# The projection weights' loads on ScalarE's DMA queue instead of SyncE's

## The chip, the cores and the metric

One core of a Trainium2 chip runs the whole kernel: TensorE (PE) multiplies, VectorE (DVE), ScalarE (ACT) and GpSimd (POOL) work beside it, and DMA transfers are issued by SyncE (SP) or ScalarE, each with a queue of its own. Every engine takes its instructions in the order in which the program gives them out. The metric is the device time of one execution in microseconds.

## The reference

One layer of a hybrid decoder block over 512 tokens of width 2048, in float32:

```python
h = _rms_norm(x, norm1_g[l])
proj = h @ w_in[l]
aq, ak, av, bu, bg, cq, ck, cv = jnp.split(proj, splits, axis=-1)
...                                   # per-head RMS norms of q and k
out_a = _dilated_mixture(aq, ak, av)  # 8 heads x 64, three dilated windows
out_b = _conformer_conv(bu, bg, ...)  # GLU, causal depthwise conv (31), LayerNorm, swish
out_c, _ = _band_attention(cq, ck, cv, C_WINDOW - 1, sinks=c_sinks[l])  # 16 q heads, 2 kv heads
x = x + jnp.concatenate([out_a, out_b, out_c], axis=-1) @ w_out[l]
h2 = _rms_norm(x, norm2_g[l])
x = x + (jax.nn.silu(h2 @ w_gate[l]) * (h2 @ w_up[l])) @ w_down[l]
```

The input projection has 3840 columns, that is 30 tiles of 128.

## The kernel before, in words

Every product is made of three: each float32 operand is split into a high part (a cast to the matmul's reduced float32, `F32R`) and the low rest, and high x high, high x low and low x high are summed in PSUM (`mm3`, L315 to L317).

**Weight units.** The weights pass through the kernel in units of 128 x 1024. A unit's way has three steps. `pump` loads it into one of a few raw buffers (`nc.sync.dma_start`, L254); `split_up_to` makes the high part with a cast on ScalarE (L286) and puts the subtraction that makes the low part into the list `lows`; `lows_now` gives that subtraction to VectorE (L264). Once a unit is split its raw buffer counts as free, and the next load into it must wait until the subtraction has read it. `next_unit` is called where PE is about to use unit u: it casts unit u + 2 (`SPLIT_AHEAD`), into one of three buffers, which PE must have released. `pump` fills raw buffers up to a limit, five of them before unit 20 (`RAW_EARLY`) and eight after (`RAW_BUFS`; seven names in use here).

**The stages.** A head part (the first four tiles, sharing the loads of x) takes the first 50 us. Then `project` makes the other 26 tiles of the input projection, two units each, in the order of `PROJ`. While PE multiplies, every second of the eight k-tiles of a unit advances a clock (`ticks.tick()`); work that was put down for a tick is given out there. In this way the attention heads, the convolution's taps (L526) and the norms run between the projections. When all tiles are made, `late` is set and the output projection begins (residual add at L1019, loads of x at L1004); after that come the gate, up and down products.

**The small transfers.** What follows a projection tile moves data across partitions through SP's queue: per-head sums of squares go out in four parts and come back (`head_scales`, L595 and L600); halves of q are copied to the other partitions, called twins (L638, L639); the scales of k go out, come back spread (L663, L669), and k's high and low parts are copied in eight transfers (L692); v goes out turned and comes back (L702, L708). On POOL, the returned sums become scales at L608 to L610, v is scaled at L713, and the heads of kind c get their probabilities spread by selects (L819, L822). Scores are at L763 and L764, transposes of probabilities at L799 (c) and L865 (a), the weighing of values at L889 and L890; ScalarE's exponentials are at L784 (c) and L838 (a), its copies out of PSUM at L578, L805, L871 and L898; VectorE's norm of kind a is at L845 to L849, its low parts at L810 and L876.

**Where a load is given out.** In `project`, `lows_now` is called at the fourth of a unit's eight k-tiles. It gives the subtraction to VectorE, and since `late_lows` is set it calls `pump` right after, so one weight load stands in SP's queue at the middle of each unit, ahead of whatever the following ticks put there. The kernel writes the order out by hand; nothing is moved by a scheduler.

Of the kernel before, what the change touches and what calls it, by code (L numbers as in the profile page):

```python
# [52 lines left out]
RAW_BUFS = 8  # L53
RAW_EARLY = 5
# [62 lines left out]
def kernel(ctx: ExitStack, tc: tile.TileContext, xT, wi, wo, wgu, wd, cst_in, outT):  # L117
    nc = tc.nc
# [22 lines left out]
    def bank(name, cols=T, pool="banks"):  # L141
        return psum[pool].tile([P, cols], F32, name=name, tag="b")
# [11 lines left out]
    def take(buf, key, n=1024):  # L154
        assert buf not in held
        held[buf] = key
        raws[key] = (wp.tile([P, 1024], F32, name=f"w{key}", tag=f"raw{buf}", bufs=1), n)
        return raws[key][0]
# [81 lines left out]
    splits = {}  # L240
    at = {"entry": 0, "split": 0, "use": 0}

    def pump(limit, most=99):
        while at["entry"] < len(entries) and len(raws) < limit and entries[at["entry"]][0] not in held and most:
            most -= 1
            buf, key, parts = entries[at["entry"]]
            if len(parts[0].shape) == 3:
                n = 4 * parts[0].shape[-1]
                nc.sync.dma_start(take(buf, key, n)[:, :n].rearrange("p (n f) -> p n f", n=4), parts[0])
                at["entry"] += 1  # L250
                continue
            t, o = take(buf, key, sum(p.shape[-1] for p in parts)), 0
            for part in parts:
                nc.sync.dma_start(t[:, o:o + part.shape[-1]], part)  # L254
                o += part.shape[-1]
            at["entry"] += 1


    lows, late_lows = [], []

    def lows_now():
        while lows:
            fn, *args = lows.pop(0)
            fn(*args)  # L264
        if late_lows:
            pump(RAW_EARLY if at["use"] <= 20 else RAW_BUFS)

    def split_up_to(i):
        while at["split"] <= min(i, len(works) - 1):
            key, last, eng = works[at["split"]]  # L270
            t, n = drop(key) if last else raws[key]
            u = at["split"]
            hi = wp.tile([P, 1024], F32R, name=f"wh{u}", tag="hi", bufs=SPLIT_BUFS)
            lo = wp.tile([P, 1024], F32R, name=f"wl{u}", tag="lo", bufs=SPLIT_BUFS)
            if eng == "moves":

                near = psum["high"].tile([P, 1024], F32R, name=f"wn{u}", tag="h")
                src = t[:, :n].rearrange("p (n f c) -> p f n c", n=4, c=P)
                by = lambda x: x[:, :n].rearrange("p (f n c) -> p f n c", n=4, c=P)
                nc.scalar.copy(by(near), src)  # L280
                nc.scalar.copy(by(hi), src)
                nc.vector.tensor_sub(by(lo), src, by(near).bitcast(F32))
            elif eng or "high" not in psum:
                eng = eng or nc.vector

                (nc.vector.tensor_copy if u == 0 else nc.scalar.copy)(hi[:, :n], t[:, :n])  # L286
                lows.append((eng.tensor_sub, lo[:, :n], t[:, :n], hi[:, :n].bitcast(F32)))
                if not late_lows:
                    lows_now()
            else:  # L290
                near = psum["high"].tile([P, 1024], F32R, name=f"wn{u}", tag="h")
                nc.scalar.copy(near[:, :n], t[:, :n])
                nc.scalar.copy(hi[:, :n], t[:, :n])
                lows.append((nc.vector.tensor_sub, lo[:, :n], t[:, :n], near[:, :n].bitcast(F32)))
                if not late_lows:
                    lows_now()
            splits[u] = (hi, lo)
            at["split"] += 1

    def sums_now():  # L300
        for fn in sums.pop(at["use"], ()):
            fn()

    def next_unit():
        sums_now()
        u = at["use"]
        at["use"] += 1
        lows_now()
        split_up_to(u + SPLIT_AHEAD)
        if not lows:  # L310
            pump(RAW_EARLY if u < 20 else RAW_BUFS, 2 if works[u][2] == "moves" else 99)
        return splits.pop(u)

    def mm3(out, wh, wl, xh, xl, start, stop):
        nc.tensor.matmul(out, wh, xh, start=start, stop=False)  # L315
        nc.tensor.matmul(out, wh, xl, start=False, stop=False)  # L316
        nc.tensor.matmul(out, wl, xh, start=False, stop=stop)  # L317
# [11 lines left out]
    for k in range(X_AHEAD):  # L329
        load_first(k)  # L330
        if k < 4 or k % 2 == 0:
            pump(k + 2 if k < 4 else k // 2 + 4)
# [109 lines left out]
    for k in range(KT):  # L442
# [5 lines left out]
        if k == 0:  # L448

            at["use"] = 2  # L450
            first = [splits.pop(u) for u in range(2)]
        elif k < 4 or k % 2 == 0:
            wh, wl = next_unit()
            o = 0
# [32 lines left out]
    def project(name):  # L487
        b = bank(name, pool="tiles")
        for half in range(2):
            wh, wl = next_unit()  # L490
            for kk in range(8):
                k = 8 * half + kk
                s = slice(kk * P, (kk + 1) * P)
                mm3(b, wh[:, s], wl[:, s], h_hi[k], h_lo[k], k == 0, k == KT - 1)
                if kk == 3:
                    lows_now()
                if kk % 2 == 1:
                    ticks.tick()
        return b
# [436 lines left out]
    mix, late = {}, []  # L936
# [34 lines left out]
    for name in PROJ[HEAD4:]:  # L971
        kind, what, j = name[0], name[1], name[2:]
        if name == PROJ[-2]:
            for n, row in enumerate(ROWS[:8]):
                ticks.after(6 + n, split_mix, row)
        b = project(name)
        if kind == "b":
            ticks.after(0, glu_u if what == "u" else glu, int(j), b)
            continue
        if kind == "c":  # L980
            box = Heads(shared) if j else shared
        else:
            box = boxes.setdefault(j, {})
        if what == "k":
            do_k(box, b, name, 1 if kind == "c" else 0)
        elif what == "v":
            do_v(box, b, name)
        else:
            do_q(box, b, name)
        if what == "q":  # L990
            if kind == "a":
                boxes.pop(j)
            attention(kind, box, mix, kind + j, (int(j), int(j) + 8) if kind == "c" else None)
# [82 lines left out]
    for half in range(2):  # L1076
        for i, n in enumerate(OUT_ORDER[half]):
            if half == 1 and i == 2:
                open_banks(banks=2, high=2)
            b = bank(f"o{half}_{n}", pool="tiles")  # L1080
            wh, wl = next_unit()
            for kk in range(8):
                k = 8 * half + kk
                row = ROWS[k]
                while row not in m_hi:
                    ticks.tick()
                s = slice(kk * P, (kk + 1) * P)
                mm3(b, wh[:, s], wl[:, s], m_hi[row], m_lo[row], kk == 0, kk == 7)
                if kk % 4 == 3 or half == 0 and kk % 2 == 1:
                    ticks.tick()  # L1090
            ticks.after(0, residual, n, b, half)
            if half == 0:
                load_x(i + 2)
        for row in ROWS[8 * half:8 * half + 8]:
            if half == 0:
                m_hi.pop(row), m_lo.pop(row)
# [263 lines left out]
    class Down:  # L1360
# [74 lines left out]
        def sum(self, i, k, a):  # L1435
            return self.g, i, k, a
# [140 lines left out]
```

## Time and profile before

| | us |
|---|---|
| median of 3 runs | 1875.88 |
| lowest and highest | 1874.54, 1877.67 |
| profiled execution | 1874.93 |
| its span | 1873.2 |
| PE busy | 1857.4 |

In rows of the profile, a line begins with its start (or, for groups, with the kernel's line), and square brackets tell how long the engine idled before it and what ended that. `wh` and `wl` are the high and low parts of a weight unit, `w` its raw buffer. Names such as `cq4d` are the data of head tile cq4 in memory, `cq4t` the same read back, `ak1h` a twin of k's high part. SPq and ACTq are the DMA issues of the two queues; the bytes move later, and a transfer's own time is given in the chain of waits as DMA.

### The profile page before, as it was taken

The page shows a single profiled execution, that of the slowest core. Times are in us where ns is not written, and L with a number is a line of the kernel's source. Part 1 is how long each engine was busy: PE and PEld are TensorE (multiplying, and loading weights), DVE is VectorE, ACT ScalarE, POOL GpSimd, SP SyncE. Part 2 cuts the span into 40 slices and gives each one's busy share as a digit, 9 for nine tenths or more (in the row PEclk, how much of TensorE's full clock was granted, in tenths as well). Part 3 has the DMA queues.
Part 4 walks back from the last instruction along what each step waited for, and adds up shares of the span by engine and source line. Part 5 has one row for each costly group of instructions (what it writes and reads, how often), then busy time and mean ns, then how long its engine had stood idle before and what let it go on. Part 6 is the DMA issues. An engine that isn't in the chain of part 4 may idle for free.

```text
span 1873.2 us, 28281 instructions
## 1 busy us (share of the span) xinstructions
PE 1857.4 (99%) x9566; PEld 1588.8 (85%) x9566; DVE 1449.9 (77%) x2295; ACT 1327.3 (71%) x1835; POOL 1155.5 (62%) x838
## 2 busy tenths in 40 slices
PE   9999999999999999999999999999999999999998
PEld 7888878877888888888888888888888888888887
DVE  6779878989689777777777777777777777777767
ACT  6355644553457888888888888888888877778775
POOL 0136543110003887877878778787777778879775
PEclk9999999999999999999999999999999999999999
DMA  7353244453333445465554655546456967666645
GB/s 271 86 153 91 85 133 118 114 142 134 115 140 113 136 159 163 153 191 168 173 162 154 194 162 174 162 154 195 148 167 235 328 215 238 216 223 230 205 136 113
DMA packets 227649, 311.34 MB, mean 166 GB/s; under 512 B 86320, under 2 KB 138672, under 8 KB 227504
## 3 DMA queue, kind: packets, MB, share of 16 engines
q1 hardware_dynamic: 227360, 309.52, 52.1%
q8 instruction: 76, 1.25, 0.3%
q14 instruction: 69, 0.57, 0.1%
q10 hardware_dynamic: 144, 0.01, 0.0%
HBM read 246.65 MB, written 54.42 MB: 161 GB/s over the span
## 4 chain that ended last, share of the span: by engine, by line
PE 89%; DVE 5%; DMA 2%; SPq 2%; POOL 1%; issue 1%; ACT 0%; POOLq 0%; DVEq 0%
PE out L1172 46%; PE out L1431 7%; PE out L1430 7%; PE out L1432 7%; PE o L315 3%; PE o L317 3%; PE o L316 3%; PE cq L315 1%; PE cq L317 1%; PE cq L316 1%; DVE wl L264 1%; PE in L315 1%; PE in L317 1%; PE in L316 1%; DVE y L526 1%
## 5 line engine op out<-in xcount | busy, mean ns | idle before, releaser
L1172 PE MATMUL out<-h,wh 128*128 128x512 f32 x2464 | 588.6, 391 | 0.0
L1172 PEld LDWEIGHTS out<-h,wh 128*128 128x128 f32 x2464 | 453.1, 188 | 87.1
L1172 PEld LDWEIGHTS out<-h,wl 128*128 128x128 f32 x2464 | 315.9, 191 | 12.0
L1172 PE MATMUL out<-h,wl 128*128 128x256 f32 x2464 | 319.7, 283 | 0.0
L1430 PE MATMUL out<-wh,a 128*128 128x512 f32 x620 | 240.6, 388 | 0.0
L1432 PE MATMUL out<-wh,a 128*128 128x512 f32 x620 | 240.6, 388 | 0.0
L1431 PE MATMUL out<-wl,a 128*128 128x512 f32 x620 | 240.6, 388 | 0.0
L286 ACT CAST wh<-w 128x1024 fp32r<-128x1024 f32 (+2 forms) x94 | 96.8, 1031 | 123.2 <-PE o L316 54.9
L264 DVE TENSOR_TENSOR wl<-w,wh 128x1024 fp32r<-128x1024 f32 (+2 forms) x95 | 113.6, 1196 | 34.2 <-ACT wh L286 34.0
L1430 PEld LDWEIGHTS out<-wh,a 128*128 128x128 f32 x620 | 116.5, 188 | 23.8
L1432 PEld LDWEIGHTS out<-wh,a 128*128 128x128 f32 x620 | 116.5, 188 | 23.8
L1431 PEld LDWEIGHTS out<-wl,a 128*128 128x128 f32 x620 | 116.5, 188 | 23.7
L1440 DVE TENSOR_TENSOR y<-y,out 128x512 f32<-128x512 f32 x164 | 106.4, 683 | 25.6 <-PE out L1432 23.7
L526 DVE SCALAR_TENSOR_TENSOR y<-bu,cst,y 128x511 f32<-128x511 f32 (+14 forms) x120 | 89.1, 743 | 0.8
L315 PE MATMUL o<-mh_c,wh 128*128 128x512 f32 x128 | 51.3, 400 | 2.5 <-DVE xr L1019 2.5
L315 PE MATMUL cq<-hh,wh 128*128 128x512 f32 x128 | 50.3, 393 | 0.0
L317 PE MATMUL o<-mh_c,wl 128*128 128x512 f32 x128 | 50.0, 391 | 0.0
L316 PE MATMUL o<-ml_c,wh 128*128 128x512 f32 x128 | 50.0, 390 | 0.0
L316 PE MATMUL cq<-hl,wh 128*128 128x512 f32 x128 | 49.9, 390 | 0.0
L317 PE MATMUL cq<-hh,wl 128*128 128x512 f32 x128 | 49.9, 390 | 0.0
L182 POOL TENSOR_TENSOR w('s', 'g0')_5692<-w('21', 'g0')_5538,w('22', 'g0')_5536 128x1024 f32<-128x1024 f32 x1 | 2.5, 2454 | 68.9 <-DVE wl L264 68.9
L431 POOL TENSOR_TENSOR lvr<-lvv,nhalf 128x4 f32<-128x4 f32 x1 | 1.9, 1920 | 67.9 <-DVE lvv L430 67.9
(3052 smaller groups left out, 4949.6 us busy)
## 6 DMA issues: line engine op xcount, KB each, us to landing
od<-a SPq DMA_DIRECT2D x154, 256.0 KB
a<-od SPq DMA_DIRECT2D x154, 256.0 KB
w<-in_wi SPq DMA_DIRECT2D x58, 512.0 KB
w<-in_wo SPq DMA_DIRECT2D x32, 512.0 KB
x<-in_xT SPq DMA_DIRECT2D x16, 256.0 KB
xr<-in_xT SPq DMA_DIRECT2D x16, 256.0 KB
x2d<-xr SPq DMA_DIRECT2D x16, 256.0 KB
z<-x2d SPq DMA_DIRECT2D x64, 64.0 KB
```

The source lines that it names most:

```text
L182: nc.gpsimd.tensor_add(out[:, :n], raws[key[a]][0][:, :n], raws[key[b]][0][:, :n])
L264: fn(*args)
L286: (nc.vector.tensor_copy if u == 0 else nc.scalar.copy)(hi[:, :n], t[:, :n])
L315: nc.tensor.matmul(out, wh, xh, start=start, stop=False)
L316: nc.tensor.matmul(out, wh, xl, start=False, stop=False)
L317: nc.tensor.matmul(out, wl, xh, start=False, stop=stop)
L526: nc.vector.scalar_tensor_tensor(yconv[j][:, i:], hconv[j][:, :T - i], c, yconv[j][:, i:], op0=ALU.mult, op1=ALU.add)
L1172: nc.tensor.matmul(out, lhs[:, s], rhs, start=begin, stop=x is xs[-1] and low == flip[0], skip_group_check=True)
L1430: nc.tensor.matmul(b[:, lo:hi], x[:, high], wh[:, s], start=start, stop=False, skip_group_check=True)
L1431: nc.tensor.matmul(b[:, lo:hi], x[:, high], wl[:, s], start=False, stop=False, skip_group_check=True)
L1432: nc.tensor.matmul(b[:, lo:hi], x[:, low], wh[:, s], start=False, stop=last, skip_group_check=True)
L1440: getattr(eng, op)(t, t, src)
```

## The change

In `project`, `next_unit` is called with ScalarE's queue. It then pumps at once, before the cast of unit u + 2, and gives the loads to ScalarE's queue; the pump at the middle of the unit is left out until `late` is set. The head part and the stages after the projections load through SP as they did, and every small transfer stays on SP's queue.

```diff
-    def pump(limit, most=99):
+    def pump(limit, most=99, queue=nc.sync):
...
             for part in parts:
-                nc.sync.dma_start(t[:, o:o + part.shape[-1]], part)
+                queue.dma_start(t[:, o:o + part.shape[-1]], part)
...
             fn(*args)
-        if late_lows:
-            pump(RAW_EARLY if at["use"] <= 20 else RAW_BUFS)
+        if late_lows and late:
+            pump(RAW_BUFS)
...
-    def next_unit():
+    def next_unit(queue=None):
         sums_now()
         u = at["use"]
         at["use"] += 1
+        if queue:
+            pump(RAW_EARLY if u < 20 else RAW_BUFS, queue=queue)
         lows_now()
         split_up_to(u + SPLIT_AHEAD)
-        if not lows:
+        if not queue and not lows:
             pump(RAW_EARLY if u < 20 else RAW_BUFS, 2 if works[u][2] == "moves" else 99)
         return splits.pop(u)
...
         for half in range(2):
-            wh, wl = next_unit()
+            wh, wl = next_unit(nc.scalar)
```

## The prediction

> **What bounds the kernel now.** I read the profile's page first, its busy times: one engine fills the span.
>
> ```profile
> PE 1857.4 (99%) x9566; PEld 1588.8 (85%) x9566; DVE 1449.9 (77%) x2295; ACT 1327.3 (71%) x1835; POOL 1155.5 (62%) x838
> ```
>
> So only PE's idle time can be won, 1873.2 - 1857.4 = 15.8 us, and only that of the stage the change touches. Next, the busy times by stretch (start:end, length, then PE, PEld, DVE, ACT, POOL).
>
> ```profile
> 62.00:224.00 162.00, 161.40 (x812) 136.81 (x812) 131.56 (x254) 83.41 (x183) 66.74 (x102) 1.00 0.37 107
> 224.00:430.00 206.00, 197.35 (x970) 164.41 (x969) 173.93 (x389) 99.55 (x189) 59.20 (x90) 1.00 0.45 124
> 430.00:545.00 115.00, 115.00 (x531) 95.43 (x530) 89.68 (x163) 51.64 (x83) 1.92 (x1) 1.00 0.37 131
> ```
>
> The projections with the attention heads between them fill 62 to about 400 us. PE idles 0.6 us in the first stretch, 8.65 us in the second and none in the third. At most 9.2 us, 0.5% of the time, can be won. The view of waits on PE names all of it (us, times, longest):
>
> ```profile
> PE o L315 <- DVE xr L1019: 2.5, 2, 1.6
> PE c7o L890 <- POOL c7pl L822: 2.1, 2, 1.8
> PE c4o L890 <- POOL c4pl L822: 1.8, 2, 1.3
> PE c6s L763 <- DMA cq<-cq6l: 1.2, 1, 1.2
> PE a1o L890 <- DVE a1pl L876: 1.0, 1, 1.0
> PE c0s L764 <- DMA ckl<-cklo: 0.6, 1, 0.6
> ```
>
> None of them is a wait for weights. What the change can shorten stands in SP's own waits in the same stage, where a weight load (L254) is held until VectorE has subtracted from the buffer that it overwrites, with every small transfer behind it held too:
>
> ```profile
> SPq L254 <- DVE wl L264: 109.9, 24, 7.9
> ```
>
> **The change part by part.**
>
> **Small transfers freed, c7.** The chain of waits and the timelines of SP, POOL and VectorE show how the 2.1 us at c7o come about.
>
> ```profile
> 222.32 1.51 DMA ak2d<-ak2p
> 226.19 3.23 DMA ak2t<-ak2d
> 239.64 3.68 DMA cq4t<-cq4d
> ```
>
> ```profile
> 225.65 0.35 SPq L254 DMA_DIRECT2D w<-in_wi  x1
> 239.00 0.53 SPq L254 DMA_DIRECT2D w<-in_wi  x1
> ```
>
> ```profile
> 229.49 0.20 POOL L608 TENSOR_TENSOR ak2wide<-ak2t 128x8 f32<-128x8 f32 x1 [1.67 <-DMA ak2t<-ak2d]
> 243.39 0.29 POOL L608 TENSOR_TENSOR cq4r<-cq4t 128x8 f32<-128x8 f32 x1 [7.59 <-DMA cq4t<-cq4d]
> ```
>
> ```profile
> 232.74 0.21 DVE L657 STREAM_TRANSPOSE ak2wide<-ak2wide 128x32 f32<-128x32 f32 x1 [0.90 <-POOL ak2wide L610]
> ```
>
> The write ak2d has landed at 222.32 + 1.51 = 223.83, but its reading back starts at 226.19, behind a weight load. Without it the read starts 2.4 us earlier. POOL can use 1.67 us of that (its idle time) and VectorE 0.9 (its own). From VectorE's transpose on, SP issues back to back up to cq4t, and a second weight load sits in front of that: 239.64 - 239.00 = 0.64 us more. Issued 1.5 us earlier, cq4t also lands sooner: 3.68 us behind 512 KB, 1.51 for a transfer without them, so 0 to 2.2 off. I take 1.2, nearer to the 3.23 and 3.68 of this kind of read. POOL, which stood 7.59 us for it, then hands c7pl over 2.7 us (1.5 to 3.7) earlier, and the stall of 2.1 is gone: **-2.1** (bounds -1.5 and -2.1). The second stall at c4o (1.8 - 1.3 = 0.5) hangs on the read of cq6 with one weight load ahead, the same form: **-0.5**.
>
> **c4 and c6.** The first stall at c4o has another releaser.
>
> ```profile
> 277.19 0.41 POOL L819 TENSOR_SCALAR_AFFINE_SELECT c4pl<-c4lp 128x256 fp32r<-128x256 f32 x1 [2.66 <-PE c4t L799]
> 279.22 1.27 POOL L822 TENSOR_SCALAR_AFFINE_SELECT c4pl<-c4lp 128x128 fp32r<-128x128 f32 x1
> 280.52 1.10 SPq L692 DMA_DIRECT2D ak0l<-ak0lo  x2
> ```
>
> POOL waited for a PE transpose there, not for SP, and then needed 3.3 us for four selects (277.19 to 280.49), which at 0.41 each would be 1.6. The end of these released SP's L692, behind which the twins of cq6 were issued, and so the 1.2 us at c6s. Both go only if POOL runs its selects faster beside an idler VectorE. From 0 to -1.3 - 1.2 = -2.5: half, **-1.2**.
>
> **What ACT takes over.** ACT gets one weight issue a unit, some 50.
>
> ```profile
> 0.80 0.40 ACTq L321 DMA_DIRECT2D cst<-in_cst  x1
> ```
>
> At 0.40 us each that is 20 us in 340, on an engine busy for 183 of the 368 us of the first two stretches; it lies in time in which ACT waits for PE to release the cast's buffer. I count it **0**; without that cover each cast would start 0.4 later, still a unit or more ahead of its use. The loads themselves leave later than now, at the unit boundary instead of at its middle, but by the limit of five buffers a load for unit u+6 goes out at boundary u and is cast at boundary u+4, some four units of 5 to 7 us later: **0**. After the last projection one load of the output weights falls behind two loads of x on SP, with seven buffers ahead of it: **0**.
>
> **The wait on VectorE.** The issue waits for the subtraction of unit u+1 and stands ahead of the cast of u+2. It bites where the subtraction ends after the cast now starts, for example
>
> ```profile
> 373.64 1.22 DVE L264 TENSOR_TENSOR wl<-w,wh 128x1024 fp32r<-128x1024 f32 x1
> 374.44 1.06 ACT L286 CAST wh<-w 128x1024 fp32r<-128x1024 f32 x1 [2.37 <-PE av L316]
> ```
>
> 374.86 against 374.44: with the issue the cast slips 0.8 us, and PE reads its result only two units later. **0**.
>
> **The wait on other transfers.** In the trace's records each transfer carries one of eight completion semaphores in turn, whichever queue issues it, and an issue waits until the transfer eight places earlier in the program has landed. The waits of SP in the first 50 us show it on loads that share no data:
>
> ```profile
> SPq L326 <- DMA w<-in_wi: 6.0, 8, 0.9
> ```
>
> On SP this costs little, as its own queue is in order. On ACT it means that a weight issue, and every cast and exponential behind it, waits for a small transfer of SP. I counted eight back at each unit boundary in program order. Mostly that transfer has landed long before; where eight k twins precede the boundary (unit contents: eight L692, four L595, two L638/L639) it is the seventh twin. The worst place is the boundary at 334 us:
>
> ```profile
> 333.32 1.94 SPq L692 DMA_DIRECT2D ak1h<-ak1hi  x2
> 338.18 1.15 SPq L692 DMA_DIRECT2D ak1l<-ak1lo  x2
> ```
>
> ```profile
> 100.48 2.36 DMA ckl<-cklo
> ```
>
> ```profile
> 334.06 1.05 ACT L286 CAST wh<-w 128x1024 fp32r<-128x1024 f32 x1
> 335.06 0.78 ACT L838 ACTIVATE a0e<-a0s,a0d,aq0r 128x512 f32<-128x512 f32 x1
> 342.56 0.59 ACT L871 CAST a0ph<-a0t 128x512 fp32r<-128x512 f32 x1 [0.98 <-PE a0t L865]
> ```
>
> ```profile
> 338.81 1.22 DVE L264 TENSOR_TENSOR wl<-w,wh 128x1024 fp32r<-128x1024 f32 x1
> 339.94 0.69 DVE L845 SCALAR_TENSOR_TENSOR a0e<-a0e,mult_a 128x512 f32<-128x512 f32 x1
> 348.92 0.16 DVE L832 SCALAR_TENSOR_TENSOR a1d<-a1d,aq1r 128x2 f32<-128x2 f32 x1 [1.47 <-POOL aq1r L610]
> ```
>
> The seventh twin goes out at 338.18 and, at a twin's 2.36 us, lands at 340.5. So ACT stands from 334.1 to 340.5; issue and cast put the cast's end at 342.0. VectorE needs it for its subtraction at 338.81: 3.2 us of new idle time, on an engine that has next to none for the rest of the stage:
>
> ```profile
> 350.00:400.00 50.00, 48.89 (x240) 40.86 (x240) 48.72 (x127) 26.24 (x46) 6.90 (x9) 1.00 0.34 94
> ```
>
> (VectorE is the third engine, 48.72 us of 50.) The exponential behind the cast feeds L845, which comes right after. Against this VectorE's present idle 1.47 us at 348.92, a wait for the read of aq1 behind a weight load, is absorbed: 3.2 - 1.47, **+1.8** on the chain that ends in PE's waits for a1pl and xr (bounds -1.5, if ACT does not wait, and +3.2, if the read gains nothing). Eight k twins stand ahead of another boundary too:
>
> ```profile
> 275.98 1.05 ACT L286 CAST wh<-w 128x1024 fp32r<-128x1024 f32 x1
> 285.51 1.23 DVE L264 TENSOR_TENSOR wl<-w,wh 128x1024 fp32r<-128x1024 f32 x1 [2.47 <-ACT wh L286]
> ```
>
> Its seventh twin is the one at 280.52 above, landing at 282.9: ACT would stand for up to 6.9 us. Here VectorE catches up in the 2.47 us that it idles at the next subtraction, and PE's next need of it is beyond that: **0**. VectorE's pause there is also what would leave POOL undisturbed in the c4 term.
>
> **A burst at c0.** At one boundary the allowance goes from five buffers to all, and three loads go out together.
>
> ```profile
> 99.46 1.06 ACT L286 CAST wh<-w 128x1024 fp32r<-128x1024 f32 x1 [1.84 <-PE cq L316]
> 103.68 5.81 SPq L254 DMA_DIRECT2D w<-in_wi  x4
> ```
>
> Now these follow the k twins on SP's queue. On ACT they start at about 100, beside the twins that PE awaits at c0s, and the load before them beside the spreading of k's scales. A read behind 512 KB took 3.23 us, a transfer with none ahead 1.51, so 1.7 more; at two places of the chain that is 0 (no contention) to +3.4. Sharing costs less than standing behind, so I take a little under half: **+1.5**.
>
> Here a page speaks against the likely gain. The Trainium skill, "DMA: Bandwidth & Descriptors", section "Queues, rings and completion order", says that each DMA engine serves the rows that have work in turns, packet by packet. By that rule a second row lets weights in among small transfers that went ahead of them before; without it this term would be 0 and the sum 1.5 lower. No row of this trace has two rows loaded at once.
>
> **Sum:** -2.1 - 0.5 - 1.2 + 1.8 + 1.5 = -0.5 us. The profiled execution took 1874.93 us, its span 1873.2 and 1.7 around it; that gives 1874.4. The median of the runs is 0.95 above the profiled one: **1875.4 us**.
>
> **The rivals.**
>
> *A clean gain.* If the eight semaphores are dealt out per queue, or SP's early start lets the twins land in time, ACT stands for nothing. Then c7 and c4's second -2.6, c4 and c6 -1.2 to -2.5 (take -1.7), the VectorE chain -1.5, c0 +0.8: -5.0, 1870.9 us. For it: the 109.9 us that SP was held. Against it: the single ACT issue took the first number of the same series.
>
> *ACT held by SP's transfers.* Slower, one mechanism at the boundaries behind k twins, at 334 us. The exponential ends at 335.84 and is used at 339.94: once ACT stands for more than these 4.1 us, something is late for certain, and it need not stop at VectorE's 3.2. Behind the exponential ACT empties banks that PE writes next (L898, L871); if these slip by the whole wait, PE stands for 6.4 - 0.6 = 5.8 us in place of the 1.8. (0.6 is what I allow PE as slack, the 0.59 of one such copy.) That makes +3.5 with the rest of the sum, and 1.2 more if POOL's selects stay slow: +4.7, 1880.6 us.
>
> *Only the issue time is saved.* If what holds the small reads is their own producers, each chain gains only the issues ahead of it: 0.35 and 0.64 at c7, the 0.5 at c4, 0.6 at aq1, and nothing else moves: -2.1, 1873.8 us. The Trainium skill, the same page, section "Issuing engines are not separate DMA queues", states just this: a second issuer saves only the sequencer's time. The row of 109.9 us speaks against it, as SP's time there is waiting, not issuing.
>
> **How the numbers follow.** A measurement of this kernel tells about 0.2%, 3.75 us, from no change: faster means under 1872.1, slower over 1879.6. My forecast has 0.43, its own range 1872.5 to 1878.5. Clean gain 0.20; ACT held 0.27; only issue time 0.10. Faster 0.20, same 0.43 + 0.10 = 0.53, slower 0.27. The range 1870 to 1881 reaches past the centres of the outer cases and leaves out about half of the clean gain's and a third of the slower case's spread.
>
> **What would show it.** Right: weight issues on ACT's queue at each boundary; SP's long wait for L264 gone from the projections; no PE wait for c7pl; an ACT wait of several us ahead of the cast near 334, released by a k twin; new VectorE idle time at the subtraction behind it; a longer wait at c0s. Wrong: no ACT wait released by a DMA (clean gain), PE idle at the a0 transposes beyond 3 us (slower case), or any PE wait for wh or wl, which would mean that weights themselves come late.

## The result, and the profile after

The changed kernel takes 1880.3 us in the median (1876.76 to 1886.69), the kernel before 1872.91 us (1871.29 to 1877.67), each over 20 executions. The ratio is 1.0037, with a 95% interval of 1.0029 to 1.0045: the change makes the kernel about 7 us slower, where the prediction had -0.5 and held no change for the likeliest. The profiled execution of the changed kernel took 1876.83 us (span 1874.7) and is among its fastest; that of the kernel before, 1874.93 us, was above its median. The two profiles therefore lie only 1.9 us apart, and they have to be read by stage.

Below is the busy line of the changed kernel's page, then its busy times by stretch, with the same columns as ahead of the prediction (start:end, length, PE, PEld, DVE, ACT, POOL, granted clock, DMA share, GB/s).

```profile
PE 1859.7 (99%) x9566; PEld 1590.1 (85%) x9566; DVE 1450.8 (77%) x2295; ACT 1327.9 (71%) x1835; POOL 1154.0 (62%) x838
```

```profile
62.00:224.00 162.00, 157.70 (x776) 133.06 (x775) 126.14 (x238) 81.00 (x179) 65.00 (x98) 0.98 0.37 111
224.00:430.00 206.00, 201.11 (x997) 168.07 (x996) 178.26 (x397) 102.16 (x192) 59.89 (x94) 1.00 0.46 126
430.00:545.00 115.00, 115.00 (x529) 95.44 (x530) 89.63 (x167) 50.62 (x82) 1.92 (x1) 1.00 0.38 133
```

TensorE now idles 4.3 us in the first stretch, where it idled 0.6, and 4.9 in the second, where it idled 8.65. What was won in the second is lost in the first. New beside that is the clock column: 0.98 in a stretch that had 1.00. The view of waits on PE names the idle time. The change adds two lines to the file, so before's L315, L764, L822 and L890 are now L317, L766, L824 and L892.

```profile
PE c0s L765 <- DMA ckh<-ckhi: 2.6, 1, 2.6
PE c0s L766 <- DMA ckl<-cklo: 1.7, 1, 1.7
PE c4o L892 <- POOL c4pl L824: 1.2, 2, 0.7
PE o L317 <- ACT a2ph L873: 1.0, 1, 1.0
PE o L317 <- DVE xr L1021: 0.9, 1, 0.9
PE c6s L765 <- DMA cq<-cq6l: 0.9, 1, 0.9
PE a1s L765 <- DMA aq<-aq1l: 0.5, 1, 0.5
PE a1o L892 <- DVE a1pl L878: 0.3, 1, 0.3
```

The stall at c7o is gone, those at c4o, xr, c6s and a1o are smaller, and TensorE stands 4.3 us for k's twins at c0s where it stood 0.6. Two small waits are new, for a2ph and at a1s. The timelines of ScalarE and SP (start, length, engine, line) show what lies between.

```profile
97.16 2.00 ACTq L254 DMA_DIRECT2D w<-in_wi  x3
```

```profile
97.75 1.12 SPq L694 DMA_DIRECT2D ckh<-ckhi  x2
100.07 1.10 SPq L694 DMA_DIRECT2D ckl<-cklo  x2
101.22 1.31 SPq L694 DMA_DIRECT2D ckh<-ckhi  x2
103.07 1.11 SPq L694 DMA_DIRECT2D ckl<-cklo  x2
```

In program order the three loads stand behind the twins in both kernels. On SP's queue that order holds, and they left at 103.68. ScalarE is held by nothing there, so on its queue they leave from 97.16 on: the first starts ahead of all the twins, and all three ahead of the low ones. The chain of waits gives the second of k's low twins a transfer of 6.19 us, where it took 2.36:

```profile
100.58 6.19 DMA ckl<-cklo
```

The DMA view of 98 to 104 us says who had the engines (queue, packets, MB, share of the 16 engines' time; q10 is ScalarE's queue, q1 SP's):

```profile
q10 hardware_dynamic: 391, 1.47, 85.0%
q1 hardware_dynamic: 158, 0.26, 13.9%
```

And the busy times in stretches of 2 us behind the stall show a second loss (the third number from the right is the granted clock):

```profile
102.00:104.00 2.00, 0.30 (x2) 0.00 (x0) 1.20 (x2) 0.00 (x0) 0.00 (x0) 1.00 1.06 307
106.00:108.00 2.00, 1.10 (x4) 1.13 (x5) 0.08 (x1) 0.00 (x0) 0.00 (x0) 0.50 0.73 173
110.00:112.00 2.00, 2.00 (x7) 1.52 (x6) 0.00 (x0) 0.00 (x0) 0.00 (x0) 0.50 0.00 0
114.00:116.00 2.00, 2.00 (x11) 1.64 (x10) 1.55 (x2) 1.98 (x4) 0.00 (x0) 1.00 0.75 238
```

After the pause TensorE runs at half speed, in the trace's record of the clock for 6.83 us, which costs half of that, 3.4 us. The profile of the kernel before has no such stretch until its last few microseconds. Over all executions the mean granted clock is 0.9972 after the change and 0.9988 before it (35 executions beside the first experiments). The difference, 0.0017 of 1873 us, is 3.1 us: nearly half of the loss is clock.

### The profile page after: what moved, and what is told of

It is laid out like the page before. It is cut to its first block, busy times and chain, and to the rows that moved or that the text cites. A ratio compares the mean times of both kernels' runs of the same rounds, so it can differ in the third digit from the quotient of the medians.

```text
span 1874.7 us, 28278 instructions
## 1 busy us (share of the span) xinstructions
PE 1859.7 (99%) x9566; PEld 1590.1 (85%) x9566; DVE 1450.8 (77%) x2295; ACT 1327.9 (71%) x1835; POOL 1154.0 (62%) x838
## 4 chain that ended last, share of the span: by engine, by line
PE 91%; DVE 5%; DMA 2%; SPq 1%; issue 1%; POOL 0%; ACT 0%; ACTq 0%; DVEq 0%
PE out L1174 46%; PE out L1433 7%; PE out L1434 7%; PE out L1432 7%; PE o L317 3%; PE o L319 3%; PE o L318 3%; PE cq L317 1%; PE cq L318 1%; PE cq L319 1%; DVE wl L264 1%; PE in L319 1%; PE in L317 1%; PE in L318 1%; DVE y L528 1%
## 5 line engine op out<-in xcount | busy, mean ns | idle before, releaser
L317 PE MATMUL o<-mh_c,wh 128*128 128x512 f32 x128 | 51.2, 400 | 2.0 <-ACT a2ph L873 1.0
L317 PE MATMUL cq<-hh,wh 128*128 128x512 f32 x128 | 51.2, 400 | 0.0
```

## The experiments

**One load per boundary.** The loads stay on ScalarE's queue, but three no longer leave together.

```
-            pump(RAW_EARLY if u < 20 else RAW_BUFS, queue=queue)
+            pump(RAW_EARLY if u < 20 else RAW_BUFS, 2 if u in (24, 28, 32) else 1, queue)
```

> Loads on ScalarE's queue as in the changed kernel, but one load per unit boundary (a second one at units 24, 28 and 32) instead of three together at c0. Theory (the burst at c0 delays the k twins by about 3.7 us, and TensorE's clock is halved for 7 to 12 us behind that pause): PE's wait at c0s under 1.5 us, no half-speed stretch near 105, the gains at c7 and c4 stay; 1866 to 1870 us, faster than the kernel before. Rival (loads on a second queue delay SP's small transfers all along, the burst is only the most visible place): c0s wait still over 2 us or other waits in its place, 1877 to 1881 us.

Measured: 1874.59 us, ratio to the kernel before 1.0002 (0.9991 to 1.0012). The wait at c0s is 0.7 us, there is no half-speed stretch there, and between 98 and 104 us the twins' queue moves 0.75 MB instead of 0.26:

```profile
q1 hardware_dynamic: 447, 0.75, 51.7%
q10 hardware_dynamic: 144, 0.52, 27.5%
```

So without the burst there is no loss that can be told from none; the interval leaves room for some 2 us. But the theory's 1866 to 1870 us did not come: without the burst the change is worth nothing that can be measured. Its gains are missing too.

> The kernel with one load per boundary, unchanged, for a second profile. Three profiles of the kernel before showed TensorE idle for 4.6, 6.2 and 8.7 us between 224 and 430 us. Theory (the change gains little there on average, the first profile of before was an unlucky one): 4.5 to 6.5 us idle here again, c0s wait under 2.5 us. Rival (the change makes these stalls dependably small): 5 us or less, with no wait over 1.2 us.

The second profile of this kernel (1874.62 us) has TensorE idle for 6.9 us between 224 and 430 us, 2.4 of them at a1s, against 5.1 in the first. The rival's dependably small stalls are not there.

**The burst two units later** (`u < 22` in place of `u < 20`).

> As the changed kernel, with the jump of the allowance from five to all buffers at unit 22 instead of 20, so that the three loads leave behind the k twins. Theory (place of the burst decides): c0s wait as in the kernel before (about 0.6 us), clock 1.000, 1866 to 1870 us; a stall of its own is possible if the three loads meet the transfers of cq3 near 119 us, with up to 3 us. Rival (a burst on a second queue costs wherever it is put, by the bytes it moves): a stall of 3 to 4 us near 110 to 120 us, 1877 to 1881 us.

Measured: 1873.35 us, ratio 1.0006 (0.9995 to 1.0018), 0.8 us at c0s. In its timeline the loads leave one by one from 107 us on, so no new burst was made. The run doesn't show what a burst would cost elsewhere; it only confirms that there is no loss without three loads at c0.

**Filler in the stall.** Twenty matmuls of constant data ahead of c0's first scores.

```
-    b = idle = None
+    b = None
...
                 b = banks[u] = bank(f"{name}s{h}{u}")
+                if name == "c0" and h == 0 and u == 0:
+                    for i in range(20):
+                        nc.tensor.matmul(b, idle, idle[:, None, :].to_broadcast([P, NT, P]), start=True, stop=True)
```

> The changed kernel with 20 matmuls of constant data (4.5 us of TensorE) ahead of the first scores of c0; their result is overwritten. Theory (the half-speed stretch follows from TensorE's pause): TensorE stays busy while the twins come, granted clock 1.00 around 105 us, the stall of 4.3 us stays as filler time; 3.4 to 6 us below the changed kernel, 1874 to 1877 us. Rival (the clock falls for another reason, for example the load on memory): the half-speed stretch stays at 105 to 112 us and the time is that of the changed kernel or more, 1880 to 1884 us.

Measured: 1877.5 us, ratio 1.0023 (1.0012 to 1.0033), and the clock stays up in the stretch around c0. Here is its row:

```profile
96.00:125.00 29.00, 29.00 (x139) 22.58 (x138) 19.09 (x38) 11.60 (x25) 4.41 (x6) 1.00 0.55 154
```

The mean clock of its executions is 0.9989, that of the kernel before. The stall's time is still spent, on filler, but 0.14%, some 2.6 us, comes back against the changed kernel's 1.0037 (the two intervals overlap slightly). The same three loads leave together here, from 98.49 on, and no half-speed stretch comes; it thus follows from TensorE's pause and not from the load on memory; the gain lies a little under the 3.4 to 6 us expected.

**The burst alone.** The kernel before, with only the pump at unit 20 moved to the boundary and to ScalarE (`pump` takes its queue as in the change).

```
...
         at["use"] += 1
+        if u == 20:
+            pump(RAW_BUFS, queue=nc.scalar)
         lows_now()
```

> The kernel before, with only the three loads at unit 20 issued on ScalarE's queue at the boundary; all other loads stay on SP. Theory (the burst alone is the loss): c0s wait 3.5 to 4.5 us, half-speed stretch behind it, none of the gains at c7 and c4; the time goes up by 7 to 10 us, 1880 to 1883 us, as slow as the changed kernel or slower. Rival (the loss needs all loads on the second queue): within 2 us of the kernel before, 1871 to 1875 us.

Measured: 1877.71 us, ratio 1.0025 (1.0013 to 1.0036). Two loads, not three, left early, and these are its waits at c0s and its clock. (The scores don't read `w`. They wait here for several semaphores, that of the high twin among them, and the view names the one that came last.)

```profile
PE c0s L765 <- DMA w<-in_wi: 2.0, 1, 2.0
PE c0s L766 <- DMA ckl<-cklo: 1.5, 1, 1.5
```

```profile
96.00:125.00 29.00, 25.43 (x112) 20.89 (x112) 18.05 (x37) 10.68 (x20) 2.93 (x3) 0.94 0.57 172
```

Two loads in the wrong place cost 4.7 us with every other load left on SP. That is less than the 7 to 10 us expected, as the burst was smaller, and far from the rival's nothing.

**The kernel before, profiled again.** These two runs asked why the gains were missing.

> The kernel before, unchanged, for a second profile. Spreading the burst brought the time back to that of the kernel before, not below it, so the 3 to 5 us forecast for c7, c4 and VectorE's chain are in question. Theory (those stalls were large by chance in the one profiled execution): TensorE idles under 6 us between 224 and 430 us instead of 8.65, c7o waits under 1.5 us, the span is 1868 to 1872. Rival (the stalls are always there, and the changed kernel trades them for others of equal size): 8 to 9 us idle, c7o near 2.1, span 1872 to 1874.

> The kernel before, unchanged, for a third profile; the same two cases as for the second look. If second and third differ by more than 2 us in TensorE's idle time between 224 and 430 us, the stalls vary from execution to execution, and one profile can't price them better than that.

Measured: 1878.84 and 1872.56 us. TensorE's idle time between 224 and 430 us, 8.65 us in the first profile, is 6.2 and 4.6. The waits of the second profile:

```profile
PE c0s L764 <- DMA ckl<-cklo: 2.0, 1, 2.0
PE c7o L890 <- POOL c7pl L822: 1.8, 2, 1.4
PE c4o L890 <- POOL c4pl L822: 1.0, 2, 0.5
```

and of the third, whose list has no c7o at all:

```profile
PE c0s L764 <- DMA ckl<-cklo: 1.7, 1, 1.7
PE c4o L890 <- POOL c4pl L822: 0.9, 2, 0.5
```

The stalls wander by 4 us from one execution to the next, and the first profile was an unlucky one. The mean of the three is 6.5 us. Six profiles with the loads on ScalarE at the boundary, the heads in their old places and k's twins on SP have 4.9, 5.1, 5.4, 5.7, 6.8 and 6.9, 5.8 in the mean. That leaves under a microsecond for the change, within the scatter. c0s shows something else: it waited 0.6 us in the first profile, 2.4 (with 0.4 for ckh) and 1.7 in the others, with a half-speed stretch behind both of the longer waits, though the twin's transfer took 2.35 and 2.36 us there. The place stood at its limit before anything was changed.

**The queue alone.** The loads stay in the middle of the unit, behind the low parts, but ScalarE issues them (`pump` takes its queue as in the change).

```
...
-            pump(RAW_EARLY if at["use"] <= 20 else RAW_BUFS)
+            pump(RAW_EARLY if at["use"] <= 20 else RAW_BUFS, queue=nc.sync if late else nc.scalar)
```

> The kernel before with the projections' loads left in the middle of the unit, only issued by ScalarE instead of SP. The burst then leaves behind the k twins. Theory (the loss is the burst's place, not the queue): c0s wait under 1 us, 1870 to 1874 us, the same as the kernel before. Rival (two queues at once cost by themselves): 1876 us or more.

Measured: 1887.77 us, ratio 1.0069 (1.0055 to 1.0084), the slowest of all. The theory was wrong that the burst would follow the twins here. ScalarE reaches it ahead of them again,

```profile
99.16 2.00 ACTq L254 DMA_DIRECT2D w<-in_wi  x3
```

and TensorE waits 5.9 us at c0s. Besides, ScalarE's own waits now have the subtraction in them, which in the changed kernel they have not in this stage:

```profile
ACT a1e L838 <- DVE wl L264: 11.0, 3, 4.0
ACT mix_c L898 <- DVE wl L264: 7.6, 3, 4.4
ACT L784 <- DVE wl L264: 6.9, 2, 6.0
ACT c7e L784 <- DVE wl L264: 4.8, 1, 4.8
```

Issued right behind the subtraction it waits for, a load holds ScalarE's exponentials (a1e, c7e) and copies. The place at the boundary is what keeps the wait on VectorE at nothing.

**The place alone.** The changed kernel with `next_unit(nc.sync)`: the boundary, but SP's queue.

> The changed kernel with its loads at the unit boundary, but issued by SP. The three loads of the burst then stand ahead of the k twins in the same queue. Theory (1.5 MB ahead of the twins is what delays them, on whichever queue): c0s wait 4 us or more, half-speed stretch behind it, SP again held by VectorE's subtraction; 1880 to 1886 us. Rival (only sharing between two queues delays the twins): c0s wait under 2 us, 1872 to 1876 us.

Measured: 1875.48 us, ratio 1.0006 (0.9995 to 1.0018). The theory's premise fell, not the mechanism: SP's program order has the loads behind the twins, and SP kept it.

```profile
105.11 1.24 SPq L694 DMA_DIRECT2D ckl<-cklo  x2
106.39 2.03 SPq L254 DMA_DIRECT2D w<-in_wi  x4
```

Same boundary, same bytes, one queue: no loss that can be told from none. Its profile has 2.7 us of waits at c0s, near the 0.6 to 2.4 of the kernel before, and the twin's transfer takes 2.36 us. It takes the second queue for the loads to pass the twins.

**Two loads at c0** (one at unit 21, two at all others).

> The changed kernel with two loads instead of three at unit 20, one at 21 and two at 22. Theory (bytes ahead of the twins decide): the c0s wait lies between that of one load (0.7 us) and of three (4.3 us), about 2 to 3 us, with a half-speed stretch behind it in most executions; 1875 to 1878 us. Rival (any second transfer on the other queue is as bad as three): the wait is 4 us again and the time 1879 to 1881.

Measured: 1879.9 us, ratio 1.0041 (1.0029 to 1.0054). The wait, 2.5 + 0.5 us, is what the theory expected of it; the time is the rival's. The clock column explains the profiled execution: 0.88 between 96 and 125 us, as much lost as with three loads (0.88), after a shorter pause. The theory's measure, the bytes, does show in the twin itself. The second low twin took 2.35 to 2.42 us wherever at most one load had left just ahead (the kernel before three times, one load per boundary twice, the later burst, the place alone), 4.86 and 5.00 with two (this run and the burst alone), 6.19 and 6.54 with three (the changed kernel and the queue alone). The time does not follow the bytes in the same way.

**High twins on ScalarE's queue**, on top of one load per boundary.

```
-                for to, part in zip(box["k"][h], parts):
+                for to, part, q in zip(box["k"][h], parts, (nc.scalar, nc.sync)):
                     for at in HALF:
-                        nc.sync.dma_start(to[at].bitcast(F32), part[HALF[h]].bitcast(F32))
+                        q.dma_start(to[at].bitcast(F32), part[HALF[h]].bitcast(F32))
```

> One load per boundary, and besides the four twins of k's high part leave on ScalarE's queue, which makes that part itself, so that SP has four issues of 0.6 us less before k's low part and before the transfers of the next q. Theory (with the burst gone the waits left at c0s, c6s and a1s, 0.7 + 0.9 + 1.1 us, hang on SP's issue time): these waits fall under 0.5 us each, the half-speed stretches behind them go, 1869 to 1873 us, 1 to 4 below the kernel before. Rival (they hang on the data's own arrival, or ScalarE's casts slip by the issues): 1873 to 1877 us, no better than one load per boundary alone.

Measured: 1875.76 us, ratio 1.0016 (1.0007 to 1.0025): slower. The single load is now issued behind the high twins, beside the low ones, and the second scores wait for these:

```profile
100.53 0.59 ACTq L254 DMA_DIRECT2D w<-in_wi  x1
```

```profile
PE c0s L766 <- DMA ckl<-cklo: 4.3, 1, 4.3
```

Without a burst TensorE waits 4.3 us here, as long as with three loads that start before the twins. The high twins and the load share ScalarE's queue in this run, and which of them holds the low twins was not separated.

**c0's scores later.** If TensorE's early arrival is the whole loss, moving the scores in its order should recover it with the burst in place.

```
             head_at[0] = t0 + every
+            if mi == "c0" and h == 0:
+                t0 += 4
```

> The changed kernel, burst and all, with the scores of c0's first head placed four ticks (24 matmuls, 5.4 us) later in TensorE's order, so that projection matmuls fill the time in which the twins come. Theory (the whole loss is TensorE reaching c0's scores before the twins, plus the halved clock that follows): c0s wait under 0.5 us, no half-speed stretch behind it, 5 to 7 us below the changed kernel, 1873 to 1876 us. Rival (the burst also delays other transfers, or a second queue costs elsewhere): the stall moves to the next waits, 1878 us or more.

Measured: 1873.7 us, ratio 1.0010 (0.9999 to 1.0020). Against the changed kernel's 1.0037 that is 0.27%, 5 us, back. TensorE is busy throughout and the clock is full:

```profile
96.00:125.00 29.00, 29.00 (x141) 24.45 (x140) 22.61 (x46) 15.25 (x33) 4.76 (x6) 1.00 0.61 178
```

The rival has a part too: in the profiled execution c6s now waits 4.9 us and a1s 2.3. The same step without the burst (three ticks), and in the kernel before:

> One load per boundary, and the scores of c0's first head three ticks (4.1 us) later. Theory (with the burst gone, the 0.7 to 1.2 us left at c0s and the half-speed stretches behind it are all that this place can still give): 1 to 3 us below one load per boundary alone, 1870 to 1873 us. Rival (later scores only push the softmax of c0 into the next stage): 1874 to 1877 us.

> The kernel before with the scores of c0's first head three ticks (4.1 us) later: the same step without any change of queue. Theory (c0s waits of 0.6 to 2.4 us were in the kernel before as well, with a half-speed stretch in two of its three profiles): 1 to 4 us below the kernel before, 1869 to 1872 us. Rival (the same knock-on as in the previous run): 1873 to 1876 us.

Measured: 1870.89 and 1870.77 us, ratios 0.9994 (0.9985 to 1.0003) and 0.9995 (0.9986 to 1.0004). These are the lowest medians, but neither can be told from the kernel before, and the queue makes no difference between them.

**Three heads later.** c0, c6 and a1 at once, with the loads on ScalarE's queue (one per boundary) and with them on SP's.

```
+            if h == 0:
+                t0 += {"c0": 3, "c6": 4, "a1": 2}.get(mi, 0)
```

> One load per boundary, and the first head's scores later at the three places where TensorE still meets a transfer: c0 by three ticks (4.1 us), c6 by four (5.4 us), a1 by two (2.7 us). Theory (what is left between 224 and 430 us is TensorE arriving at c6s and a1s before the twins of q, 0.9 to 4.9 and 0.5 to 2.5 us, with halved clock behind the longer ones): no wait over 1 us at these three, no half-speed stretch before the end, 1867 to 1870 us, 0.1 to 0.3% below the kernel before. Rival (the time saved is met by the next wait, VectorE's and GpSimd's work at c4, xr and the outputs of a1): 1870 to 1873 us.

> The kernel before, loads on SP, with the same three heads later. Theory (these waits belong to both kernels, so the queue makes no difference once TensorE doesn't wait for them): the same time as with the loads on ScalarE's queue within 2 us, 1867 to 1870 us. Rival (SP's held queue delays c7 and c4 as the prediction had it, and the change is worth 3 to 5 us once the burst is out of the way): 3 us or more slower than the kernel with one load per boundary.

Measured: 1875.48 us, ratio 1.0010 (1.0001 to 1.0018), and 1875.14 us, ratio 1.0012 (1.0003 to 1.0022). Both are slightly slower than the kernel before, by 2 us, and both time forecasts failed, but the comparison is clear: with the waits at c0s, c6s and a1s gone, the two queues give the same time. The waits moved on to GpSimd's selects in both; the first row is of the one, the second of the other:

```profile
PE c4o L892 <- POOL c4pl L824: 5.4, 3, 4.6
```

```profile
PE c4o L890 <- POOL c4pl L822: 4.6, 2, 4.2
```

No version beat both kernels by more than a measurement can tell.

## Why the prediction was wrong

**The step that failed: the burst at c0.** The prediction saw that three loads would start at about 100 us beside the k twins, and gave it +1.5 us, at most +3.4. It sized the term by one load: a read behind 512 KB had taken 1.7 us longer. The burst is three times that, and it does not merely share with the twins but starts ahead of them, at 97.16. The wait at c0s grew by 3.7 us in the profiled execution, above the upper bound. The sum then had no term at all for what TensorE does after a pause: 3.4 us lost at half speed in that profile, 3.1 in the mean of all executions (from the mean clocks). The place and the kind of wait were right; with the clock, the term of +1.5 measured about 7. That this place is the loss was shown from three sides: spreading the loads removes it, two of them, put alone into the kernel before, cost 4.7 us, and moving the scores recovers 5 us with the burst in place.

**The gains at c7, c4 and VectorE's chain.** In the one profile after they look as forecast: no wait for c7pl (-2.1 forecast), and c4o 1.2 in place of 1.8, c6s 0.9 in place of 1.2, a1o 0.3 in place of 1.0, xr 0.9 in place of 2.5. They were priced, though, from one execution, in which they were large. In the second and third profiles of the kernel before, c7o waits 1.8 and not at all, and it is missing from three more profiles with nearly all loads on SP in the middle of the unit (the burst alone, and the kernel before with later scores, twice). So its absence after the change is no sign of a gain. With the burst gone the time is 1.0002 of that of the kernel before (0.9991 to 1.0012), and with the waits of c0s, c6s and a1s out of the way the queues are equal. SP's 109.9 us behind the subtraction were time in which the small transfers could mostly wait: in the changed kernel SP stands for their producers instead, up to 29.9 us at a time. That is the third rival's claim, that these producers hold the chains. The Trainium skill, "DMA: Bandwidth & Descriptors", section "Issuing engines are not separate DMA queues", states that a second issuer saves only the sequencer's time; the equal times 1875.48 and 1875.14 agree, as far as a gain goes; the loss came from the order that the second queue gave up. In the prediction's sum the -3.8 of these gains thus measured as nothing that can be told.

**The wait on other transfers (+1.8) did not occur.** The timeline of ScalarE at the place named:

```profile
336.79 0.37 ACT L873 CAST a0ph<-a0t 128x256 fp32r<-128x256 f32 x1 [0.15 <-PE c6o L892]
336.85 0.35 ACTq L254 DMA_DIRECT2D w<-in_wi  x1
337.25 1.05 ACT L286 CAST wh<-w 128x1024 fp32r<-128x1024 f32 x1
```

The issue goes out at once and the cast follows. The eight semaphores are shared by both queues, as the prediction read them, but in the trace their numbers run on nearly in the order in time of the issues (997 of 1058 steps from one issue to the next lead to the next number; in the kernel before all do), not in the order in which the program's loop writes them. By its number the load at 336.85 stands behind seven of the k twins and ahead of aq1's small transfers. It took the number that the load of 328.87 had had, and ScalarE did not stand for that. I had counted eight places back in the loop and hit the seventh twin. (The term was also 1.7 rather than 1.8: 3.2 - 1.47.) The slower rival, built on the same wait, fell with it; the time came out near its 1880.6 us for another reason.

**What held.** ScalarE's issues cost nothing, as forecast: one load per boundary is level with the kernel before. The loads that leave later made TensorE wait for no weights in the projections. The wait on VectorE is nothing at the boundary; the queue alone, in the middle of the unit, showed what it costs elsewhere. The longer wait at c0s was on the list of what would show the forecast right, so the sign of that term was there and its size decided.

**The base.** The forecast started at 1875.9 us, the median of three executions; over 20 the kernel before takes 1872.91. In 1875.4 us the error of the base hides part of that of the sum: -0.5 forecast, about +7 measured.

## What to carry to other kernels

A queue that issues in order is also a priority: before moving bulk transfers to a second queue, look for the place where it kept them behind small ones that an engine awaits, and size that place by all the bytes that can now pass. The time need not follow them in proportion: two loads cost 0.41% in one run, three 0.37%. Price a pause of TensorE by its length and by the half-speed stretch behind it. A stall read from one execution is worth what it is in several; take a second profile before counting it as a gain.

## What the runs showed of the hardware

Pauses of TensorE of about 1.7 us were enough to halve its clock. The third profile of the kernel before shows it, with a pause of 1.7 us at 102.5 to 104.2 and the clock falling at 105.7:

```profile
102.00:104.00 2.00, 0.48 (x3) 0.19 (x2) 1.97 (x3) 0.00 (x0) 0.69 (x1) 1.00 0.81 174
106.00:108.00 2.00, 2.00 (x6) 1.55 (x5) 0.00 (x0) 0.00 (x0) 0.00 (x0) 0.50 0.94 289
```

The half-speed stretches before the end of the kernel were 3.41 or 6.83 us long in every trace, never anything between, and each began a whole number of steps of 3.413 us after the first entry of its trace's clock record. Cut into these steps, the 18 traces agree on what decides. Each of the 17 stretches followed a step in which TensorE, by its rows, idled for 1.74 us or more in total, about half of the step, and no step at full speed with 1.73 us or less was followed by one. So the same pause costs clock or none by where it falls: the 1.74 us of the third profile at c0s lay within one step, while the 2.4 us at a1s in the second profile with one load per boundary were cut into 1.73 and 0.65 and cost none. A second step at half speed came where TensorE idled for 0.6 us or more in the first, and did not with 0.48 or less. That is why 3.0 us (two loads, 2.01 and then 0.98) cost 6.83 us of half speed, and both the 3.5 us of the burst alone (its last 0.12 in the second step) and the 4.3 us of the run with the high twins on ScalarE's queue (nothing in the second) cost 3.41. The rule was read from these traces; no run was made to test it.

The Trainium skill, "TensorE: Matmul & The Clock Gate", Part 1, describes a free-running window of 3413 ns, which agrees with the step of 3.41. The advice of the Trainium skill on the same page, section "Why this matters for your kernels", to leave no idle gaps over some 3 us, is too wide for this kernel, where 1.74 us was enough, and the measurement decides.
